# First layer's modulation vectors by unsplit float32 matmuls on column quarters, tokens loaded first

## The chip, the core and the metric

The kernel runs on one core of a Trainium2 chip. The metric is device time in microseconds, from the first to the last instruction of one launch. A core has TensorE (PE, with its weight loads listed apart as PEld), VectorE (DVE), ScalarE (ACT), GpSimd (POOL) and queues that move data from DRAM; here nearly all loads are issued by SyncE (SP).

## The reference, cut to what matters

Two transformer layers (the second of another kind than the first) are followed by two blocks with experts. Only the start of the first layer and its attention matter here. `c` and `c_ctx` are two vectors of 1024; `ada_w[i]` is 1024 x 6144. The six modulation vectors of a layer are a matrix product with only two rows:

```python
c_act = silu(c); cc_act = silu(c_ctx)
mx = split(c_act @ ada_w[i] + ada_b[i], 6)      # for the 512 tokens x
mc = split(cc_act @ ada_w[i] + ada_b[i], 6)     # for the 256 places of the context
h_x = rms_norm(x, norm1_g[i]) * (1 + mx[1]) + mx[0]
h_c = rms_norm(y_ctx, norm1_g[i]) * (1 + mc[1]) + mc[0]
out_c, out_x = windowed_gqa_sink(h_x, h_c, attn_w_qkv, ...)
x = x + mx[2] * out_x                           # mx[3], mx[4], mx[5] serve the feed-forward part
```

So nothing of the first layer's products can start before vectors 1 (scale) and 0 (shift) are there; vectors 2, 4 and 3 are needed later, in and behind the attention.

## The kernel before

All activations stand with features on the partitions: `x` is a tile of 128 x 8 x 512, `ctxT` one of 128 x 8 x 256, and tokens are worked on in groups of 256 (two of `x`, one of the context). Nearly all products are exact in float32 by splitting both operands into a high and a low float32r part (`split`: ACT makes the high part, L299, DVE the low part, L300) and adding three products of parts (L351 to L353 in `mm3`, L956 to L958 in `Attention.product`).

One `ada_w` vector (`ada_pe`, from L461) is made in two halves of 512 columns. For each half eight matmuls, one for each 128 rows of `ada_w`, take the activated vectors as the stationary operand and 128 x 512 weights as the moving one. There are two forms. With `split=True` the weights are split, the stationary operand has four columns (high and low part of both vectors, `csp`), and the matmuls are L478 and L479. With `split=False` the weights stay float32 and the stationary operand has two columns (L473). The profile shows each float32 matmul as two matmul instructions, one pass each; the program gives both forms an array shape of 128 rows by 32 columns at column 0. The result row is copied out by ACT (L482), turned by four transposes (L485), and the bias is added (L490 to L493).

At the start (from L1516) the order written is: load and compute the scale vector (chunk 1) in the split form, then issue the loads of the tokens (L1535) and the context (L1536), then the shift vector (chunk 0) in the split form with the squares and the sums of the three groups' norms between its steps (`squares` L593 and L595, `rstds` L605 to the spread at L393). When the shift vector is copied out (`take`, L1480), `Norm.gen` runs for each group and each of 8 feature tiles: a multiplication by gain and 1/rms (L623), the high part (L624), and the low part, for even tiles by L629, for odd tiles by a second pass on ACT (L626) and L627. `Attention.begin` runs beside it: it loads the first keys' and queries' weights, splits them and runs the first keys' and queries' products (`firstk`, `firstq`, `firstc`), one group after the other.

The attention then runs over 8 pairs of heads with 6 blocks each (`Attention.heads`). Between the steps of a block it takes steps of other work from a queue (`Fill.pump`), each step giving its length by `yield` (0.9 for one L473 matmul). The queue orders by rank: token values, keys, the next pair's queries, output projections (added in pairs 2, 4 and 6), and last the modulation vectors: both halves of vector 2 in pair 0, one half each of vectors 4, 4, 3, 3 in pairs 1, 3, 5, 7. The share of the queue taken in each block (`rate`) counts 7.6 for each such half. What an engine runs at which place is in the end set by a scheduler that goes by the order of writing and by when operands are ready in its own estimate.

Of the kernel before, what the change touches and what calls it, by code (L numbers as in the profile page):

```python
# [18 lines left out]
S = 512  # L19
# [75 lines left out]
def _constants():  # L95
# [22 lines left out]
    # attention rope: head_dim 64 = [r1 16 | r2 16 | c1 16 | c2 16], two heads on the partitions  # L118
# [12 lines left out]
    # window mask, keys [previous block | own | next]  # L131
# [4 lines left out]
    # retention rope: 64 row frequencies | 64 column frequencies  # L136
# [4 lines left out]
    # retention decay exponents  # L141
# [7 lines left out]
    # partial rope of the second block  # L149
# [11 lines left out]
    # pooling counts  # L161
# [6 lines left out]
    # hyena: position features, decay window, transform tables  # L168
# [15 lines left out]
    # forward [n, (cos f 0..511 | -sin f 0..511, with the Nyquist column in place of f=0)]  # L184
# [30 lines left out]
# ---------------------------------------------------------------------------  # L215
# device side
# ---------------------------------------------------------------------------
class Net:
# [22 lines left out]
    # -- small tables -------------------------------------------------------  # L241
# [14 lines left out]
    # -- weights ------------------------------------------------------------  # L256
# [27 lines left out]
    def more(self, pairs, stages=0):  # L284
        """further buffers for weights"""
# [7 lines left out]
    def split(self, v):  # L293
        """f32 [128, k, c] -> hi, lo (f32r), exactly v = hi + lo up to float32's last bit"""
# [8 lines left out]
    # -- streams beside the main one, by the time of the tensor engine -------  # L303
# [13 lines left out]
    def side(self, gen, steady=False):  # L317
        """a generator whose steps each take so long; steady: on the whole, else each of them at least"""
# [12 lines left out]
    def cpanel(self, src, k, c, some=slice(None)):  # L331
        """[128, k, c] from DRAM, as pieces of 128 columns"""
# [3 lines left out]
    def kpanel(self, src, k, c):  # L336
        """[128, k, c] from DRAM, as pieces [128, 1, c]... of at most 1024 elements, listed by k"""
# [9 lines left out]
    # -- products -----------------------------------------------------------  # L347
# [15 lines left out]
    def rsqrt(self, pool, v, n):  # L363
        """[128, n] small: 1 / sqrt(v)"""
# [4 lines left out]
        # a first guess from the exponent and three steps of Newton's  # L369
# [11 lines left out]
    def col_stats(self, ps, sq, scale, eps, pool):  # L381
        """sums of sq [128, n] over the partitions -> scale * sum + eps, tokens on the partitions [128, n / 128]"""
# [7 lines left out]
    def spread(self, ps, y, pool):  # L390
        """y [128 tokens, nb] -> the same on all partitions, tokens along the free axis, in ps [128, nb * 128]"""
# [53 lines left out]
# -- first block -------------------------------------------------------------  # L445
# [4 lines left out]
class Hidden:  # L450
    """the normalized inputs of a layer in two parts (hi, lo), features on the partitions: tokens, then context"""
# [9 lines left out]
def ada_pe(net, i, chunk, mod, stage, row, halves=(0, 1), done=None, split=True):  # L461
    """one of the six modulation vectors, for both streams, on the tensor engine, by split weights or in float32"""
    nc = net.nc
    src = net.ins["ada_w"][i].rearrange("(k p) c -> p k c", p=128)
    n = 4 if split else 2
    for j in halves:
        acc = net.ps()[:n]
        for k in range(8):
# [3 lines left out]
            if not split:  # L472
# [3 lines left out]
            if k % 2 == 0:  # L476
                h, l = net.split(w[:, k % 4:k % 4 + 2])
# [2264 lines left out]
```

## Time and profile before

| | us |
|---|---|
| median of 3 runs | 3169.13 |
| lowest and highest | 3168.89, 3169.7 |
| profiled execution, span | 3174.9 |
| first product of the attention starts (in the profiled execution) | 44.83 |
| first scores start | 91.5 |
| last pair of heads begins | 411.1 |

The profiled execution is one run of its own; its span is 5.8 us above the median. Over the whole span PE is busy 95%, DVE 64%, ACT 44%.

How to read the rows further down. A row of stretches has the stretch, its length, then for PE, PEld, DVE, ACT and POOL the busy time and the number of instructions, then the granted TensorE clock (1.00 is 2.4 GHz, 0.50 is 1.2 GHz), the DMA engines' busy share and GB/s. A row of the timeline has start, duration, engine, line, operation, output<-inputs, shapes, count (merged neighbours) and, in brackets, idle time before it and what ended it. A row of grouped instructions has line, engine, operation, names, shapes, count, then busy time, mean ns of one, and the idle time before them with its causes. Matmuls overlap in their pipeline, so their spacing is read from starts, not from durations.

### The profile page before, as it was taken

The numbers are of one execution on the slowest core, as the hardware profiler recorded it, in microseconds if no ns is written. First come the engines' busy times: TensorE is split into PE (matmuls) and PEld (weight loads), VectorE is DVE, ScalarE is ACT, GpSimd is POOL, SyncE is SP. The second block draws the span as 40 slices with busy tenths as digits, with TensorE's granted clock in tenths as the row PEclk, the third lists the DMA queues.
The fourth block names the chain that finished last, engine by engine and source line by source line (L and its number), as shares of the span: only waits on it lengthen the run. The fifth ranks groups of instructions, "written<-read, shape, count | busy, mean of one in ns | idle before, by whom it ended". The sixth has DMA issues, their size and how long they took to land. (4 is left out here: it accounts for less than half of the span.)

```text
span 3174.9 us, 45357 instructions
## 1 busy us (share of the span) xinstructions
PE 3008.7 (95%) x17640; PEld 2541.3 (80%) x17640; DVE 2021.1 (64%) x3944; ACT 1398.8 (44%) x2431; POOL 375.7 (12%) x362
## 2 busy tenths in 40 slices
PE   7999999999999999999999999989989989999996
PEld 4777779888888988888887788877878867788874
DVE  7688886445552754535465543668778666977865
ACT  6567773121212532323343322436555544645544
POOL 0011130000000200000010000211213211121211
PEclk8999999999999999999999999999999989999997
DMA  6112123334441222313133332231469943145994
GB/s 218 61 48 66 47 74 100 120 100 126 134 146 54 86 69 77 92 53 93 61 103 105 128 121 90 83 117 46 122 199 360 336 157 119 41 136 200 376 349 156
DMA packets 316336, 410.38 MB, mean 129 GB/s; under 512 B 15374, under 2 KB 263310, under 8 KB 314960
## 3 DMA queue, kind: packets, MB, share of 16 engines
q1 hardware_dynamic: 305744, 369.61, 35.5%
q0 software_dynamic: 10368, 37.75, 3.1%
q8 instruction: 144, 2.36, 0.3%
q14 instruction: 80, 0.66, 0.1%
HBM read 379.01 MB, written 28.31 MB: 128 GB/s over the span
## 5 line engine op out<-in xcount | busy, mean ns | idle before, releaser
L299 ACT ACTIVATE hi<-st 128x1024 fp32r<-128x1024 f32 (+1 forms) x436 | 449.7, 1035 | 637.6 <-PE ps L352 490.1
L300 DVE TENSOR_TENSOR lo<-st,hi 128x1024 fp32r<-128x1024 f32 (+1 forms) x436 | 531.6, 1222 | 197.7 <-ACT hi L299 191.8
L351 PE MATMUL ps<-hxh,hi 128*128 128x512 f32 (+1 forms) x1280 | 477.7, 374 | 5.0 <-DVE ctxT L756 2.1
L352 PE MATMUL ps<-hxl,hi 128*128 128x512 f32 (+1 forms) x1280 | 475.1, 371 | 0.3 <-DVE hxl L629 0.3
L353 PE MATMUL ps<-hxh,lo 128*128 128x512 f32 (+1 forms) x1280 | 474.4, 371 | 0.0
L351 PEld LDWEIGHTS ps<-hxh,hi 128*128 128x128 f32 x1280 | 241.9, 189 | 54.6 <-ACT sg L809 5.3
L353 PEld LDWEIGHTS ps<-hxh,lo 128*128 128x128 f32 x1280 | 242.1, 189 | 42.4 <-issue 1.2
L352 PEld LDWEIGHTS ps<-hxl,hi 128*128 128x128 f32 x1280 | 242.4, 189 | 40.8 <-issue 1.2
L351 PE MATMUL ps<-ah,hi 128*128 128x256 f32 (+1 forms) x592 | 200.7, 339 | 3.1 <-DVE x L756 1.9
L352 PE MATMUL ps<-al,hi 128*128 128x256 f32 (+1 forms) x592 | 198.7, 336 | 0.2 <-DVE al L361 0.2
L353 PE MATMUL ps<-ah,lo 128*128 128x256 f32 (+1 forms) x592 | 198.5, 335 | 0.0
L756 DVE SCALAR_TENSOR_TENSOR x<-ps,vecs,x 128x512 f32<-128x512 f32 (+1 forms) x136 | 84.4, 623 | 144.4 <-PE ps L353 144.0
L2517 PE MATMUL pa<-hi,xt 128*128 128x256 f32 x576 | 168.0, 292 | 0.6 <-ACT xt L360 0.5
L2519 PE MATMUL pa<-lo,xt 128*128 128x256 f32 x576 | 164.7, 286 | 0.0
L2518 PE MATMUL pa<-hi,xt 128*128 128x256 f32 x576 | 163.8, 284 | 0.0
L810 DVE TENSOR_TENSOR sg<-sg,ps 128x512 f32<-128x512 f32 (+1 forms) x70 | 40.0, 572 | 190.9 <-PE ps L353 190.6
L351 PEld LDWEIGHTS ps<-ah,hi 128*128 128x128 f32 x592 | 111.6, 189 | 19.7 <-DVE x L756 5.1
L351 PE MATMUL ps<-hi,hxh 128*128 128x256 f32 x416 | 120.9, 291 | 3.7 <-DVE hy L1953 1.1
L2543 PE MATMUL py<-st,at 128*128 128x512 f32 x272 | 122.7, 593 | 1.3 <-DVE y L2547 1.3
L352 PE MATMUL ps<-lo,hxh 128*128 128x256 f32 x416 | 119.8, 288 | 2.2 <-DVE lo L300 2.2
L352 PEld LDWEIGHTS ps<-al,hi 128*128 128x128 f32 x592 | 111.6, 189 | 12.5 <-DVE al L361 0.4
L353 PEld LDWEIGHTS ps<-ah,lo 128*128 128x128 f32 x592 | 111.5, 188 | 12.5
(651 smaller groups left out, 7755.3 us busy)
## 6 DMA issues: line engine op xcount, KB each, us to landing
st<-moe_w_dram SPq DMA_DIRECT2D x102, 1024.0 KB, 10.7
st<-ffn_w_in_dram SPq DMA_DIRECT2D x44, 1024.0 KB, 5.3
ast<-ada_w_dram SPq DMA_DIRECT2D x56, 512.0 KB, 4.6
st<-ret_w_qkvg_dram SPq DMA_DIRECT2D x24, 1024.0 KB, 5.2
st<-ffn_w_out_dram SPq DMA_DIRECT2D x24, 768.0 KB, 4.8
st<-ada_w_dram SPq DMA_DIRECT2D x12, 1024.0 KB, 5.2
st<-w_in_dram SPq DMA_DIRECT2D x12, 1024.0 KB, 7.5
ast<-ada_w_dram SPq DMA_DIRECT2D x8, 1024.0 KB, 12.6
```

The source lines that it names most:

```text
L299: self.nc.scalar.activation(h, v, AF.Copy)
L300: self.nc.vector.tensor_tensor(l, v, h.bitcast(F32), op=OP.subtract)
L351: self.nc.tensor.matmul(ps, wh, xh, start=(i == 0), stop=False)
L352: self.nc.tensor.matmul(ps, wh, xl, start=False, stop=False)
L353: self.nc.tensor.matmul(ps, wl, xh, start=False, stop=(i == n - 1))
L756: net.nc.vector.scalar_tensor_tensor(xm, p, self.gate[:, m:m + 1], xm, op0=OP.mult, op1=OP.add)
L810: nc.vector.tensor_tensor(sg, sg, pu, op=OP.mult)
L2517: nc.tensor.matmul(o, th[:, k], wh[:, kk], start=(k == 0), stop=False)
L2518: nc.tensor.matmul(o, tl[:, k], wh[:, kk], start=False, stop=False)
L2519: nc.tensor.matmul(o, th[:, k], wl[:, kk], start=False, stop=(k == 7))
L2543: nc.tensor.matmul(py[:, n * 512:n * 512 + 512], at[:, f], w2[f][:, 0, n * 512:n * 512 + 512], start=(f == 0), stop=(f == 1))
```

## The change

- `ada_pe` loses the split form. A matmul takes 32 columns as its stationary operand (`cwide[k]`: the two wanted columns and 30 that follow them in the same tile) and writes to one of four quarters of the accumulator's partitions; block k of the rows goes to quarter k mod 4, so that each quarter sums two blocks. The quarters are added, and the row turned, by four float32 matmuls with a 128 x 2 matrix of ones and zeros (`sel`) in place of the transposes. All halves of vectors 1, 0, 2, 4 and 3 are made so.
- The start issues the loads of tokens and context before any of `ada_w`. Squares and sums of the norms stand before the scale vector's steps, 1/rms within them. The multiplication by gain and 1/rms (`scaled`) stands between the scale and the shift vector. Behind the shift vector each group needs only the high and the low part (`shifted`, 8 ACT and 8 DVE instructions per group; the second ACT pass of odd tiles is gone). The first keys' and queries' weights are loaded and split behind the first group.
- In the attention a step of a modulation vector counts 0.25 for a matmul and 0.8 for the end of a half, and `rate` 2.8 for a half.

The core of the diff:

```diff
-def ada_pe(net, i, chunk, mod, stage, row, halves=(0, 1), done=None, split=True):
+def ada_pe(net, i, chunk, mod, stage, row, halves=(0, 1), done=None):
...
-            if not split:
-                nc.tensor.matmul(acc, net.cact[:, k, :], w[:, k % 4], start=(k == 0), stop=(k == 7))
-                yield 0.9
-                continue
-            if k % 2 == 0:
-                h, l = net.split(w[:, k % 4:k % 4 + 2])
-            nc.tensor.matmul(acc, net.csp[:, k, :], h[:, k % 2], start=(k == 0), stop=False)
-            nc.tensor.matmul(acc, net.csp[:, k, :], l[:, k % 2], start=False, stop=(k == 7))
-            yield 0.45
+            q = k % 4 * 32
+            nc.tensor.matmul(acc[q:q + 32], net.cwide[k], w[:, k % 4], start=(k < 4), stop=(k >= 4), tile_position=(0, q))
+            yield 0.25
...
-            nc.tensor.transpose(pt[:, m * n:m * n + n], row1[:, m * 128:(m + 1) * 128], net.ident[:n, :n])
+            nc.tensor.matmul(pt[:, m * 2:m * 2 + 2], row1[:, m * 128:(m + 1) * 128], net.sel, start=True, stop=True)
...
+    def scaled(self):
+        for k in range(8):
+            self.net.nc.vector.scalar_tensor_tensor(self.sq[:, k], self.x[:, k, self.xs], self.gain[:, k:k + 1], self.r, op0=OP.mult, op1=OP.mult)
+
+    def shifted(self):
+        nc = self.net.nc
+        for k in range(8):
+            hh, hl, s = self.hh[:, k, self.xs], self.hl[:, k, self.xs], self.shift[:, k:k + 1]
+            nc.scalar.activation(hh, self.sq[:, k], AF.Identity, bias=s)
+            nc.vector.scalar_tensor_tensor(hl, self.sq[:, k], s, hh.bitcast(F32), op0=OP.add, op1=OP.subtract)
...
-            rate = (10 * (pr < 7) + 16 * (pr in (2, 4, 6)) + 10 * (pr in (2, 7)) + 7.6 * len(beside.get(pr, ()))) / 6
+            rate = (10 * (pr < 7) + 16 * (pr in (2, 4, 6)) + 10 * (pr in (2, 7)) + 2.8 * len(beside.get(pr, ()))) / 6
...
-            ns = norms(0, 0, hid, asp, sp)
-            run(ada_pe(net, 0, 1, mod, stage, row))
-            gain(0, 0)
             for hs in HS:
                 nc.sync.dma_start(x[:, :, hs], net.ins["xT"][:, :, hs])
             nc.sync.dma_start(ctxT, net.ins["cT"])
-            shift = ada_pe(net, 0, 0, mod, stage, row)
+            ns = norms(0, 0, hid, asp, sp)
             for n in ns:
                 n.squares(asp.tile([128, 8, 256], F32, name=net.nm("xsq"), tag="xsq", bufs=3))
-                for _ in range(5 if n is ns[0] else 6):
-                    next(shift)
+            scale = ada_pe(net, 0, 1, mod, stage, row)
+            for _ in range(9):
+                next(scale)
             RmsNorm.rstds(ns, sp, asp)
-            run(shift)
+            run(scale)
+            gain(0, 0)
+            for n in ns:
+                n.scaled()
+            run(ada_pe(net, 0, 0, mod, stage, row))
             take(0, 0)
+            first = []
+            for n in ns:
+                n.shifted()
+                if n is ns[0]:
+                    first += [Attention.panel(net, c) for c in (1024, 0)]
```

## Rows read from the trace of the kernel before

**Rows 1.** Head of the page: span of the profiled execution, instructions.
```profile
span 3174.9 us, 45357 instructions
```
**Rows 2.** Stretches of the start, all engines (columns as told above).
```profile
0.00:10.00 10.00, 0.59 (x1) 0.08 (x1) 1.33 (x7) 3.32 (x4) 0.19 (x4) 1.00 0.79 256
10.00:24.00 14.00, 9.73 (x39) 3.19 (x39) 10.98 (x16) 11.13 (x17) 0.00 (x0) 0.98 1.06 377
24.00:36.00 12.00, 8.57 (x28) 4.21 (x28) 11.56 (x23) 9.25 (x12) 0.00 (x0) 0.60 1.06 374
...
44.80:65.00 20.20, 17.90 (x131) 16.09 (x131) 19.47 (x49) 17.42 (x38) 0.00 (x0) 1.00 0.28 88
...
71.00:81.50 10.50, 10.24 (x50) 10.02 (x48) 7.21 (x26) 2.06 (x3) 0.50 (x1) 0.51 0.58 200
```
**Rows 3.** Groups of instructions up to 44.8 us (columns as told above).
```profile
L300 DVE TENSOR_TENSOR lo<-ast,hi 128x1024 fp32r<-128x1024 f32 x16 | 18.9, 1221 | 6.2 <-ACT hi L299 6.2
```
**Rows 4.** Timeline of the shift vector's end, up to the first product.
```profile
42.03 0.59 ACT L482 ACTIVATE arow<-ps 4x512 f32<-4x512 f32 x1 [0.32 <-PE ps L479]
...
42.67 0.41 PE L485 MATMUL ps<-kident,arow 4*128 4x4 f32 x4 [0.46 <-ACT arow L482]
...
44.07 0.24 DVE L1480 COPY vecs<-mod 128x8 f32<-128x8 f32 x2
...
44.83 0.39 PE L956 MATMUL firstk<-hxh,hi 128*128 128x256 f32 x1 [1.75 <-ACT hxh L624]
```
**Rows 5.** Groups of instructions from 44 to 69 us: the norms' parts.
```profile
L624 ACT ACTIVATE hxh<-nt,vecs 128x256 fp32r<-128x256 f32 x16 | 7.7, 503 | 4.0 <-DVE nt L623 2.3 <-DVE vecs L1480 1.6
L623 DVE SCALAR_TENSOR_TENSOR nt<-x,gains,nps 128x256 f32<-128x256 f32 x15 | 6.9, 476 | 0.0
...
L629 DVE SCALAR_TENSOR_TENSOR hxl<-nt,vecs,hxh 128x256 fp32r<-128x256 f32 x8 | 3.9, 482 | 0.0
```
**Rows 6.** Timeline: last of the norms, last of the first products, statistics behind them.
```profile
64.45 0.43 DVE L627 TENSOR_TENSOR hcl<-nt,hch 128x256 fp32r<-128x256 f32 x1 [0.46 <-ACT nt L626]
...
67.76 0.28 PE L957 MATMUL firstc<-hcl,hi 128*128 128x256 f32 x1
67.88 0.28 PE L958 MATMUL firstc<-hch,lo 128*128 128x256 f32 x1
...
68.11 0.95 PE L972 MATMUL ps<-kblk,ol 128*128 128x2 f32 x8
```
**Rows 7.** Timeline of PE around three groups of the modulation matmuls, in the attention.
```profile
120.22 0.38 PE L1183 MATMUL po<-th,vs 128*128 128x256 f32 x1
120.53 1.02 PE L473 MATMUL ps<-st,cact 128*2 128x512 f32 x2
121.48 0.38 PE L1184 MATMUL po<-tl,vs 128*128 128x256 f32 x1
...
133.45 1.88 PE L473 MATMUL ps<-st,cact 128*2 128x512 f32 x4
```
**Rows 8.** Group of the modulation matmuls over the attention, 91.5 to 459 us.
```profile
L473 PE MATMUL ps<-st,cact 128*2 128x512 f32 x96 | 47.5, 592 | 0.0
```
**Rows 9.** Stretches: pairs of heads 1, 3, 4 and 5.
```profile
137.30:178.80 41.50, 41.42 (x228) 27.43 (x227) 31.05 (x96) 30.76 (x76) 5.14 (x7) 1.00 0.24 77
...
236.10:281.70 45.60, 45.11 (x269) 34.23 (x268) 35.92 (x102) 29.00 (x71) 5.40 (x7) 1.00 0.11 36
281.70:325.20 43.50, 41.34 (x274) 36.53 (x273) 39.06 (x109) 31.60 (x77) 5.29 (x7) 1.00 0.26 86
325.20:367.70 42.50, 41.41 (x238) 29.89 (x237) 33.57 (x96) 29.25 (x75) 5.75 (x7) 1.00 0.05 13
```
**Rows 10.** Timeline: ACT and PE beside one group of the modulation matmuls.
```profile
168.99 1.88 PE L473 MATMUL ps<-st,cact 128*2 128x512 f32 x4
...
169.09 0.58 ACT L360 ACTIVATE th<-tr 128x512 fp32r<-128x512 f32 x1
...
170.80 0.39 PE L1183 MATMUL po<-th,vs 128*128 128x256 f32 x1
```

More of the change, by code (lines that the diff above doesn't have):

```diff
@@ L611, in rstds @@
             net.spread(a.r, y[:, 2 * g:2 * g + 2], pool)
-    def gen(self):
-        if self.r is None:
-            yield 1.5
-            ps = yield from self.sums()
-            yield from self.rstd(ps, self.acc, EPS)
-            self.r = ps[:, 256:512]
+    def scaled(self):
[7 more added lines that the diff above has]
+            nc.vector.scalar_tensor_tensor(hl, self.sq[:, k], s, hh.bitcast(F32), op0=OP.add, op1=OP.subtract)
+    def gen(self):
+        yield 1.5
+        ps = yield from self.sums()
+        yield from self.rstd(ps, self.acc, EPS)
+        self.r = ps[:, 256:512]
         nc, gain, shift = self.net.nc, self.gain, self.shift
@@ L946, in t, with panel @@
         return (pool or self.ap).tile(list(shape), dt, name=self.net.nm(tag), tag=tag, bufs=bufs)
-    def panel(self, c0):
-        net = self.net
-        return net.split(net.stage(self.wq[:, :, c0:c0 + 128], 8, 128))
+    @staticmethod
+    def panel(net, c0):
+        wq = net.ins["attn_w_qkv"][0].rearrange("(k p) c -> p k c", p=128)
+        return net.split(net.stage(wq[:, :, c0:c0 + 128], 8, 128))
     def product(self, p, w, c0, n, yields=True):
@@ L1015, in keys @@
     def keys(self, j):
-        w = self.panel(1024 + j * 128)
+        w = self.panel(self.net, 1024 + j * 128)
         f, sq = self.ftiles()
@@ L1052, in queries_rest, with begin @@
         yield 0.1
-    def begin(self, before, ps_es):
+    def begin(self, first, ps_es):
         net, nc = self.net, self.net.nc
-        kw, qw = self.panel(1024), self.panel(0)
+        kw, qw = first
         wst = net.stage(self.wq[:, :, 1280:1536], 8, 256)
@@ L1061, in begin @@
         for g, (c0, n) in enumerate(GR):
-            before[g]()
             for is_k, w in ((1, kw), (0, qw)):
@@ L1466, in first_block @@
     fb = es.enter_context(net.pool("first"))
-    net.cact = fb.tile([128, 8, 2], F32, name="cact")
-    nc.scalar.activation(net.cact, net.v("c2").rearrange("p (k v) -> p k v", v=2), AF.Silu)
-    net.csp = fb.tile([128, 8, 4], F32R, name="csp")
-    nc.vector.tensor_copy(net.csp[:, :, 0:2], net.cact)
-    nc.vector.tensor_tensor(net.csp[:, :, 2:4], net.cact, net.csp[:, :, 0:2].bitcast(F32), op=OP.subtract)
+    cact = fb.tile([128, 48], F32, name="cact")
+    nc.vector.memset(cact, 0.0)
+    nc.scalar.activation(cact[:, :16], net.v("c2"), AF.Silu)
+    net.cact = cact[:, :16].rearrange("p (k v) -> p k v", v=2)
+    net.cwide = [cact[:, 2 * k:2 * k + 32] for k in range(8)]
+    net.sel = fb.tile([128, 2], F32, name="sel")
+    nc.vector.tensor_reduce(net.sel, net.ident.rearrange("p (c q) -> p q c", q=32)[:, 0:2], axis=AX.X, op=OP.add)
     mods = [fb.tile([128, 6, 8, 2], F32, name=f"mod{i}") for i in range(2)]
@@ L1536, in first_block @@
             nc.sync.dma_start(ctxT, net.ins["cT"])
[L1537 removed]
+            ns = norms(0, 0, hid, asp, sp)
             for n in ns:
                 n.squares(asp.tile([128, 8, 256], F32, name=net.nm("xsq"), tag="xsq", bufs=3))
[L1540 to L1541 removed]
+            scale = ada_pe(net, 0, 1, mod, stage, row)
+            for _ in range(9):
+                next(scale)
             RmsNorm.rstds(ns, sp, asp)
[L1543 to L1544 removed]
+            run(scale)
[3 more added lines that the diff above has]
+            run(ada_pe(net, 0, 0, mod, stage, row))
+            take(0, 0)
+            first = []
[3 more added lines that the diff above has]
+                    first += [Attention.panel(net, c) for c in (1024, 0)]
         aes = ExitStack()
         att = Attention(net, hid, x, ctxT, vecs[:, 0, 1, 0], vecs[:, 0, 1, 1], fill, aes, sp)
[L1548 to L1558 removed]
+        att.begin(first, ps_es)
         def ada(ch, j):
@@ L1562, in ada @@
             row = lambda: (late.get("pool") or att.rp).tile([128, 512], F32, name=net.nm("arow"), tag="aux")
-            return lambda: ada_pe(net, 0, ch, mod, net.stage, row, (j,), done, False)
+            return lambda: ada_pe(net, 0, ch, mod, net.stage, row, (j,), done)
         ms = ExitStack()
```

30 lines of the change are left out of this document (7 added, 23 removed).

## The prediction, made before any run of the changed kernel

> **What bounds the kernel now.** I read the page's head first [rows 1], then the stretches of the start, and asked of each what is late. Up to 36 us the load queues move 256, 377 and 374 GB/s, and the DMA engines are at or near full use [rows 2]. Both vectors (8.4 MB), the tokens and the context (3.15 MB) and the small tables (0.26 MB) are 11.8 MB, and by these rates they have passed at 10 + 14 + 10.6 = 34.6 us. So the start is bound by the load first. Then comes a tail: the shift vector's row is copied at 42.03, turned at 42.67, taken at 44.07, and the first product starts at 44.83 [rows 4]. That tail is long because the weights' split lies behind the load: 16 low parts of 1.22 us on DVE [rows 3], which also sums the squares (11.56 of 12 us busy, [rows 2]). From 44.8 to 65 us DVE is the bound, 19.47 of 20.20 us [rows 2], with the norms' instructions at 476 to 482 ns each [rows 5]. PE does its products as the tiles come, and the last of 144 starts at 67.88 and ends at 68.16 [rows 6]. From there to the first scores (91.5 us) it is a chain of the kernel's own, with a stretch at half clock (0.51 from 71 to 81.5 us, [rows 2]).
>
> In the attention PE is shown busy for nearly the whole of each pair of heads, but that is not a PE at its peak. Pair 4 has no modulation matmul and a projection, 8 x (6 x 0.24 + 6 x 0.12) = 17.3 us of matmuls at the spacing of [rows 6] (0.12 us for 256 columns, twice that for 512). Pairs 1, 3 and 5 have no projection, and 8 to 13 modulation matmuls. Pair 4 takes 43.5 us, the others 41.5, 45.6 and 42.5 [rows 9]. So the side work hardly shows in the length of a pair; it sits where PE would wait for ACT and DVE. [Rows 10] show one such place: a modulation group occupies PE from 168.99 to 170.80, and the tile that the next matmul reads is only made from 169.09 to 169.67.
>
> **The change, part by part.**
>
> (1) Loads. The same 11.8 MB pass, in another order. The first piece of `ada_w` lands behind 4.5 MB, at 10 + 1.9 MB / 377 = 15.0 us, then one piece of 1.05 MB every 2.8 us, the eighth at 34.6 us. As now, weights of keys and queries are issued beside the last pieces; I take 35.2 us, and 36 as the late bound. No queue gains a wait in front of these loads: the eighth piece needs the buffer of the first, whose matmuls are done by 18 us.
>
> (2) Splits. 16 ACT and 16 DVE instructions go, 18.9 us of DVE alone [rows 3]. They pay for the multiplications that are moved forward: 24 x 0.476 = 11.4 us of DVE [rows 5] between the scale vector (ready near 26 to 27 us) and the shift vector, done at about 38 us and so hidden; if the scale vector is 3 us later, 2 us of it show.
>
> (3) The matmuls on quarters. One float32 matmul is two passes, and two matmuls in a row take 1.88 us with a last pass of 0.59, so a pass takes 0.43 and a matmul 0.86 [rows 7]. The trace of before has no two matmuls on different quarters, so what four of them cost is bounded: 4 x 0.86 = 3.44 us if nothing overlaps, 0.86 + a little = 0.95 if all four run together, and 5 x 0.43 = 2.15 if matmuls start in order and a quarter's second pass waits for its first, so that it runs beside the next quarter's first. A joint with other matmuls costs 0.31 - 0.12 = 0.19 us before a group and 0.95 - 0.86 = 0.09 behind it [rows 7], 0.28 in all. I take 2.15, the value that follows from passes issued in order; 3.44 is the slow end, and beyond it 4 x (0.86 + 0.28) = 4.56, were each quarter a joint. The Trainium skill ("TensorE: Matmul & The Clock Gate", Part 3: Packing small matmuls) says that matmuls on different column quarters run at once, 2.38 times as fast for three of them, and that matmuls start and end strictly in order; no row here shows the first. By its factor four would take 1.4 us, an estimate, instead of my 2.15.
>
> (4) The tail behind the last piece: 2.15 + 0.17 for the end of the last pass, 0.7 for the copy (0.59 and its wait, [rows 4]), four float32 matmuls with `sel`, eight passes, as long as the eight at 0.95 us [rows 6] and 0.1, then bias, two copies and the first high part, 0.2 + 0.35 + 0.55. That is 5.2 us: first product at 40.4 instead of 44.83, 4.4 us sooner (39.2 with full overlap).
>
> (5) Norms. Behind the shift vector 24 high parts on ACT (12 us at 0.50) and 24 low parts on DVE (24 x 0.48 = 11.5), plus two splits of weights (2.1 and 2.4) and small tables (0.5): done at 39.9 + 14.4 = 54.3, against 64.88 now [rows 5, 6]. Next in line is PE: 144 x 0.12 = 16.9 us of products from 40.4, 1 us for waits on the first group, so the end is near 58.3 instead of 68.16. What follows keeps its 23.4 us. **Start: 10 us gained**, of which 4.4 is (4) and the rest (5).
>
> (6) Clock. In 24 to 36 us, with PE busy 8.57 of 12, 0.60 was granted; later 71 to 81.5 fell to 0.51 [rows 2]. That stretch, about 10 us at half clock, cost 5 us of PE time. I leave it as it is; it may go (5 us gained) or another like it may fall on the first products (5 us lost). The same page of the Trainium skill ("TensorE: Matmul & The Clock Gate", Part 1) says that the clock falls after a stretch with the engine idle; by that rule the thinner use of PE under the load speaks against the change. The 5 us either way are from the row alone.
>
> (7) Attention. 48 matmuls, 96 passes [rows 8], are 41.3 us; mostly they stand alone, so with joints up to 41.3 + 48 x 0.28 = 55. After: 48 x 0.43 = 20.6, twelve groups' joints 3.4, and the four matmuls with `sel` instead of transposes, 6 x 0.6 = 3.6. PE work falls by some 25 us (35 with full overlap, 8 with none). What comes back in time is bounded by nothing and all of it. The pairs of [rows 9] say little comes back: 17.3 against some 9 us of side work, and 43.5 us against 42.5 in pair 5, is 1 us for 8, and against pair 3 less than nothing. I take a quarter, as fewer joints also shorten the waits that ACT and DVE have for PE: **6 us**. The lower `rate` spreads queries over more blocks; that side work is cheap either way, by the same rows, and I cost it at nothing, with 4 us either way if that cover is thinner than it looks.
>
> Nothing behind the attention changes but its time. Sum: 10 + 6 = 16 us. The profiled execution would go from 3174.9 to about 3159; it lies 5.8 above the median, and I carry the difference over: 3169.1 - 16 = 3153.
>
> **Rivals.** (A) No overlap of quarters. PE needs 3.44 us for a piece that comes every 2.8, so from 15.0 us it runs 8 x 3.44 = 27.5, with some 4 us of statistics and `sel` matmuls between, to 46.5; the vector is there at 49.1 and products end at 67, 1 us sooner. The attention gains 8 us of PE work, 2 of time. Time 3166. For it: no row shows overlap. (B) The side work does cost its PE time, and it all comes back: 10 + 25 to 35, 3125 to 3134. Against it stand pair 4 and [rows 10]. (C) The gain at the start is lost before the first scores: value products and statistics that now fill PE's waits up to 68 us come behind, and a clock fall hits them; 5 at the start, 3 in the attention, 3161. (D) Slower: every quarter is a joint, 1.14 us a matmul. Then the vector waits for PE: 15.0 + 36.5 + 4 + 2.6 = 58, products end at 76, 8 late, and the attention gives nothing back: 3177. It decides from (68.2 - 15.0 - 4 - 2.6 - 17.9) / 32 = 0.90 us a matmul; alone it is 0.86. "TensorEngine Tiling (Array Packing)" in the Trainium skill (Key Properties) says that changing the tiling mode drains the engine, and changing the tile alone does not; by that D would not come.
>
> **How the numbers follow.** Forecast, overlap and a quarter back, 3144 to 3161: 0.66. A 0.14, a fifth of it beyond the bound of 0.2%, which is about what a measurement of this kernel can tell from no change (6.3 us; faster is below 3162.8). B 0.07. C 0.06. D 0.07. Faster: 0.66 + 0.07 + 0.03 of A + 0.04 of C = 0.80. Slower 0.07, same 0.13. The range goes from the forecast's low end, with the clock stretch gone and some of B, 3139, up to A, 3167.
>
> **What will show it.** The first `firstk` product near 40 us (A: 49 or later; D: 58). L624 has 24 instructions and L626 none; the last of the norms near 54; the last `firstc` near 58. Four quarter matmuls in a row start 0.43 us apart or less with overlap, 0.86 without. First scores near 81. Pairs 1, 3 and 5 shorter by 1 to 2 us each, pairs 4 and 6 not; if they lose 5 each it is B. The prediction is wrong if the start's gain is gone at the first scores, or if the pairs get longer because their blocks lack side work.

## The result, and the profile after

The change made the kernel slower: 3191.89 us (median of 4 runs, 3189.77 to 3192.66) against 3169.41 for the kernel before, measured beside it. The ratio is 1.0067, 95% interval 1.0053 to 1.0081. The prediction was 3153, range 3139 to 3167, with a chance of 0.07 for slower. It was wrong in size and in sign.

Read against the rows of before, the profiled execution of after has this course. The first scores start at 84.2 us instead of 91.5, so 7.3 us were gained at the start. The last pair's last scores end at 459.6 instead of 450.4, so 16.5 us were lost in the attention. The rest adds 6.8 us more, and the span is 3190.9 against 3174.9 [rows 1]. So the two traces show 16.0 of the 22.5 us between the medians; the traced execution of before lies above its median, and where the other 6.5 us are is not shown.

**The start.** Stretches of after (stretch, length, busy time and instructions of PE, PEld, DVE, ACT, POOL, granted clock, DMA share, GB/s), to be held against [rows 2]:

```profile
24.00:36.00 12.00, 10.49 (x71) 5.56 (x75) 4.90 (x16) 1.20 (x2) 0.00 (x0) 1.00 1.06 379
36.00:44.20 8.20, 2.58 (x17) 1.79 (x9) 6.14 (x19) 2.11 (x4) 0.00 (x0) 0.67 0.15 45
44.20:49.10 4.90, 4.43 (x19) 4.13 (x20) 4.90 (x11) 4.90 (x12) 0.00 (x0) 0.50 0.66 212
```

The clock of the first row holds from 28.6 us on only, where the trace's records of the clock begin; ahead of that PE ran at the half level, as "The start alone, repaired" shows.

The timeline of after around the shift vector's end, which answers to [rows 4]:

```profile
36.86 0.60 ACT L477 ACTIVATE arow<-ps 128x512 f32<-128x512 f32 x1 [3.09 <-PE ps L474]
...
37.91 3.22 DVE L605 SCALAR_TENSOR_TENSOR xsq<-ctxT,gains,nps 128x256 f32<-128x256 f32 x8
41.04 0.16 DVE L482 TENSOR_TENSOR mod<-ps,vec 128x8 f32<-128x8 f32 x1
...
41.35 1.84 PE L480 MATMUL ps<-sel,arow 128*128 128x2 f32 x8 [4.61 <-DVE mod L482]
...
43.42 0.24 DVE L1483 COPY vecs<-mod 128x8 f32<-128x8 f32 x2
...
44.19 0.58 PE L958 MATMUL firstk<-hxh,hi 128*128 128x256 f32 x1 [1.01 <-ACT hxh L612]
```

The load is over at 36 us as forecast, and the row is copied out at 36.86, 5.2 us sooner than before. But the `sel` matmuls that turn it wait 4.61 us, and for DVE. Not for their own operand: the two accumulators of `net.ps()` take turns, and the one that they need is read by the bias addition of the first half (L482). That one stands in DVE's queue behind all 24 multiplications (L605, 31.64 to 41.13). Meanwhile PE is idle, its clock falls (0.67 from 36 to 44.2), and the first products run at the half level (0.50 from 44.2 to 49.1).

**The attention.** One row for each kernel, from the first to the last score matmuls, before and then after:

```profile
91.50:450.40 358.90, 345.60 (x2072) 268.31 (x2072) 287.20 (x804) 247.26 (x599) 49.66 (x61) 0.99 0.18 58
```

```profile
84.20:459.60 375.40, 341.48 (x2096) 280.92 (x2095) 284.55 (x803) 245.95 (x597) 48.13 (x61) 0.95 0.17 56
```

PE's idle time grows from 358.9 - 345.6 = 13.3 us to 33.9, and the granted clock falls from 0.99 to 0.95. At 0.95 over 375 us, 0.05 x 375 = 19 us of PE time are lost to the half level, against 4 before. Groups of PE instructions in these stretches show which work went and where the idle time stands (count, busy us, mean ns, idle before them and what ended it). Before:

```profile
L1183 PE MATMUL po<-th,vs 128*128 128x256 f32 x172 | 53.2, 318 | 3.7 <-ACT th L360 2.9
L1175 PE MATMUL tr<-kident,pt 128*128 128x128 f32 x344 | 49.8, 277 | 3.3 <-ACT pt L1160 3.2
L1184 PE MATMUL po<-tl,vs 128*128 128x256 f32 x172 | 48.8, 305 | 3.3 <-DVE tl L361 3.1
...
L1133 PE MATMUL sc<-maskr,identr 128*128 128x384 f32 (+1 forms) x63 | 21.8, 346 | 0.6 <-ACT pt L1145 0.5
...
L485 PE MATMUL ps<-kident,arow 2*128 2x2 f32 x24 | 2.4, 202 | 0.1
```

After:

```profile
L1184 PE MATMUL po<-th,vs 128*128 128x256 f32 x172 | 55.0, 326 | 10.6 <-ACT th L360 8.1 <-DVE ob L1202 1.6
L1185 PE MATMUL po<-tl,vs 128*128 128x256 f32 x172 | 50.6, 313 | 6.0 <-DVE tl L361 5.7
L1176 PE MATMUL tr<-kident,pt 128*128 128x128 f32 x344 | 50.5, 280 | 7.2 <-ACT pt L1161 4.8 <-DVE tl L361 1.0 <-POOL pt L1159 1.0
...
L474 PE MATMUL ps<-st,cact 128*32 128x512 f32 x96 | 24.1, 669 | 0.2 <-DMA st<-ada_w_dram 0.2
L1134 PE MATMUL sc<-maskr,identr 128*128 128x384 f32 (+1 forms) x63 | 22.5, 357 | 3.6 <-ACT pt L1146 3.4
...
L480 PE MATMUL ps<-sel,arow 128*128 128x2 f32 x48 | 6.0, 247 | 1.6 <-ACT arow L477 1.4
```

The modulation matmuls are cheaper by 47.5 [rows 8] - 24.1 = 23.4 us, the `sel` matmuls dearer than the transposes by 3.6. That is 20 us less work, near the forecast. But the waits for the attention's own chain (`pt`, then `th` and `tl`, then `ob`, made by ACT and DVE) grew by as much: for `th` from 2.9 to 8.1, for `tl` from 3.1 to 5.7, ahead of the scores from 0.5 to 3.4.

By pairs of heads, each from its first scores to the next pair's, pairs 0 to 5 take 51.0, 51.3, 51.4, 46.0, 47.3 and 44.7 us, before 45.8, 41.5, 57.3, 45.6, 43.5 and 42.5. Pairs 0 and 1 lose 15 us, pair 2 gains 6, and pair 4, which has no modulation matmul, loses 4.

What a visit of the quarter matmuls costs is seen on PE's timeline of after, from its start to the next matmul's:

```profile
145.89 1.05 PE L474 MATMUL ps<-st,cact 128*32 128x512 f32 x2
146.87 0.38 PE L1184 MATMUL po<-th,vs 128*128 128x256 f32 x1
...
148.71 1.05 PE L474 MATMUL ps<-st,cact 128*32 128x512 f32 x4
149.69 0.39 PE L1184 MATMUL po<-th,vs 128*128 128x256 f32 x1
150.01 1.06 PE L474 MATMUL ps<-st,cact 128*32 128x512 f32 x6
151.00 0.39 PE L1185 MATMUL po<-tl,vs 128*128 128x256 f32 x1
```

One, two or three matmuls (2, 4, 6 passes) all cost 0.98 to 0.99 us at the full clock. With the visits at the half clock (1.84 to 1.85 us for one matmul) and the longer ones, there are 18, 25.0 us by their starts.

### The profile page after: what moved, and what is told of

Read it like the earlier page. It is cut to its first block, busy times and chain, and to the rows that moved or that the text cites. A ratio compares the mean times of both kernels' runs of the same rounds, so it can differ in the third digit from the quotient of the medians.

```text
span 3190.9 us, 45377 instructions
## 1 busy us (share of the span) xinstructions
PE 3006.9 (94%) x17680; PEld 2557.0 (80%) x17680; DVE 2004.1 (63%) x3924; ACT 1375.8 (43%) x2403; POOL 377.5 (12%) x362
## 5 line engine op out<-in xcount | busy, mean ns | idle before, releaser
L576 POOL TENSOR_TENSOR nacc<-nacc,nsq 128x256 f32<-128x256 f32 x56 | 50.0, 892 | 605.5 <-ACT nsq L575 597.1
```

The lines of the kernel that those rows point to most:

```text
L576: nc.gpsimd.tensor_tensor(self.acc, self.acc, sq, op=OP.add)
```

## The experiments

All results together. The ratio is to the kernel before, run beside each; attention is the stretch named above, with PE's idle time and the granted clock in it. These last four columns come from one traced execution, whose own time stands under "traced" (for before only its span is known). Those of e4 and e11 are the shortest of their kernels, 8 and 7 us below the median; that of e6 is the longest, 6 us above.

| run | median us | ratio [95%] | traced | first scores | attention | idle | clock |
|---|---|---|---|---|---|---|---|
| before | 3169 to 3172 | 1 | 3174.9 (span) | 91.5 | 358.9 | 13.3 | 0.99 |
| after | 3191.9 | 1.0067 [1.0053, 1.0081] | 3192.7 | 84.2 | 375.4 | 33.9 | 0.95 |
| e1_start_only | 3173.9 | 1.0011 [1.0001, 1.0020] | 3171.7 | 84.7 | 359.2 | 12.4 | 0.99 |
| e2_attn_only | 3192.6 | 1.0069 [1.0052, 1.0085] | 3191.7 | 92.4 | 373.5 | 33.8 | 0.95 |
| e3_one_quarter | 3192.0 | 1.0063 [1.0046, 1.0080] | 3195.2 | 85.1 | 374.2 | 19.3 | 0.98 |
| e4_pad32 | 3184.6 | 1.0044 [1.0027, 1.0060] | 3176.6 | 80.3 | 374.1 | 34.4 | 0.95 |
| e5_before_shift | 3176.6 | 1.0017 [1.0007, 1.0028] | 3179.4 | 91.3 | 357.7 | 12.0 | 0.99 |
| e6_best | 3162.5 | 0.9975 [0.9965, 0.9984] | 3168.1 | 85.7 | 359.6 | 11.5 | 0.98 |
| e7_burst | 3175.1 | 1.0014 [1.0005, 1.0024] | 3174.2 | 84.0 | 364.4 | 30.7 | 0.97 |
| e8_no_mods | 3152.1 | 0.9938 [0.9920, 0.9955] | 3152.6 | 83.7 | 347.4 | 31.8 | 0.96 |
| e9_warm | 3168.0 | 0.9991 [0.9982, 1.0000] | 3170.9 | 78.7 | 358.8 | 11.8 | 0.99 |
| e10_rate | 3176.1 | 1.0020 [1.0010, 1.0029] | 3178.7 | 83.1 | 366.3 | 28.2 | 0.95 |
| e11_burst_rate | 3175.4 | 1.0019 [1.0009, 1.0028] | 3168.4 | 82.6 | 361.3 | 29.2 | 0.96 |
| e12_warm_front | 3167.7 | 0.9985 [0.9976, 0.9994] | 3168.0 | 84.9 | 359.6 | 12.8 | 0.99 |

### Either half of the change alone

e1_start_only keeps the new start and has the old matmuls (`ada_old`) and `rate` 7.6 in the attention:

```diff
-            return lambda: ada_pe(net, 0, ch, mod, net.stage, row, (j,), done)
+            return lambda: ada_old(net, 0, ch, mod, net.stage, row, (j,), done)
```

> The changed kernel's start (tokens first, quarters, first norm during the load), but the five modulation vectors of the attention are made as in the kernel before: one unsplit float32 matmul after the other on two rows, with the old rate of side work (7.6 a vector). Theory T1 (the loss sits in the attention, where the cheaper quarter matmuls leave TensorE idle and its granted clock falls): the start keeps its gain of 7 us at the first scores (84 against 91.5 us), the pairs last what they lasted before (45.8, 41.5, 57.3, 45.6, 43.5, 42.5 us), half-clock time from 92 to 490 us goes back from 44 us to 14 to 20 us, and the time is 3160 to 3166 us, faster than the kernel before by 3 to 9 us. Rival R1 (the pairs drift because everything behind the start is ordered or timed otherwise, whatever the modulation's matmuls are): pairs of 46 to 51 us, as in the changed kernel, and 3180 us or more. Rival R2 (the late part, behind 490 us, loses 7 us on its own by the shifted addresses or the clock): 3165 to 3173 us.

e2_attn_only is the kernel before with only the attention's part of the change (`ada_quarters`: quarters, `sel`, steps and `rate`):

```diff
-            return lambda: ada_pe(net, 0, ch, mod, net.stage, row, (j,), done, False)
+            return lambda: ada_quarters(net, 0, ch, mod, net.stage, row, (j,), done)
```

> The mirror image: the start of the kernel before (split weights, tokens later), and in the attention the quarter matmuls with the rate 2.8 of the changed kernel. T1: first scores at 91 to 92 us as before, pairs of 46 to 51 us, some 30 us more at half clock between 92 and 490 us than before, drift of +16 us at the attention's end, and 3180 to 3200 us. R1: pairs as before and 3165 to 3173 us. If quarters and start only lose together, both this run and the one with the start alone are near 3169 us.

e1's attention lasts 359.2 us, its six first pairs 45.8, 41.5, 55.5, 45.6, 45.9, 42.2. e2's lasts 373.5, and e2 alone has the whole slowdown (1.0069). So the loss is in the attention, and it comes with the attention's part of the change (form, steps and `rate` together), not with the start (R1 falls). But e1 is 8 to 14 us later than T1 said: the 7 us of its start are not in its time. That is nearest to R2 (3165 to 3173 us), and the next two runs took it up.

### A tile of 32 bytes

The change dropped a tile of 32 bytes per partition (`as4`) among the constants. By it the residual, the hidden pair and the weights' ring moved from addresses 32 above a multiple of 64 to multiples of 64. e4 puts a dummy of that size into after, e5 into before, where it does the reverse:

```diff
     nc.vector.memset(net.one, 1.0)
+    net.pad = cp.tile([128, 8], F32, name="pad")
+    nc.vector.memset(net.pad, 0.0)
```

> The changed kernel with a dummy tile of 32 bytes per partition among the constants, which puts the large buffers behind it back on the addresses they had in the kernel before (the change removed a tile of that size). Nothing else differs but one small memset at the start. Rival R2 (addresses): the drift of +7 us between 490 and 2050 us goes, and the time is 3183 to 3187 us. If addresses do nothing: 3189 to 3194 us, and the drift there stays, a matter of the clock that was granted.

> The kernel before with one dummy tile of 32 bytes per partition added among the constants: the same instructions but for one small memset, with the residual, the hidden pair and the weight ring at addresses that are a multiple of 64 bytes, as in the changed kernel, and no longer 32 above one. Rival R2 (the addresses are a second cost of the change, beside the attention): the first 490 us as before, then a slow drift of +7 to +10 us between 550 and 2650 us, and 3175 to 3180 us. If the addresses are nothing: 3166 to 3172 us and no drift.

Two marks on DVE's timeline, in the second layer's vectors and at the end of the retention part, bound a stretch in which all kernels run the same instructions. Before:

```profile
543.96 0.17 DVE L521 TENSOR_TENSOR mod<-ps,vec 128x8 f32<-128x8 f32 x1 [0.41 <-PE ps L519]
...
1557.34 1.28 DVE L1408 SCALAR_TENSOR_TENSOR of<-mu,of 128x512 f32<-128x512 f32 x2
```

e5_before_shift:

```profile
543.03 0.17 DVE L523 TENSOR_TENSOR mod<-ps,vec 128x8 f32<-128x8 f32 x1 [0.41 <-PE ps L521]
...
1559.77 1.28 DVE L1410 SCALAR_TENSOR_TENSOR of<-mu,of 128x512 f32<-128x512 f32 x2
```

After:

```profile
553.00 0.17 DVE L510 TENSOR_TENSOR mod<-ps,vec 128x8 f32<-128x8 f32 x1 [0.41 <-PE ps L508]
...
1569.68 1.28 DVE L1409 SCALAR_TENSOR_TENSOR of<-mu,of 128x512 f32<-128x512 f32 x2
```

The stretch lasts 1013.4 us in before, 1016.7 in e5 and 1016.7 in after. From the first mark to the last squares of that part, 1.4 us later, it is 1017.9 to 1018.1 in the four kernels with the moved addresses (after, e1, e3, e5) and 1012.8 to 1016.1 in the ten with the old ones. So the addresses do cost time, though less than the 7 to 10 us expected: 2 to 5 us in this stretch, with the granted clock at 1.00 in all fourteen, and 5.4 us (2.2 to 8.9) for e5 as timed. e4's ratio is 0.0023, or 7 us, below after's, and its 3184.6 us lie where the address rival put them. Its trace does not show where these 7 us are, for it is that of a shorter execution, whose clock was up sooner. Which of the moved buffers does it was not tried.

### The attention: clock, dose, visits, or work

e3_one_quarter lets all eight matmuls of a half sum on one quarter, so that none overlap; steps and `rate` are after's.

```diff
-            nc.tensor.matmul(acc[q:q + 32], net.cwide[k], w[:, k % 4], start=(k < 4), stop=(k >= 4), tile_position=(0, q))
+            nc.tensor.matmul(acc[:32], net.cwide[k], w[:, k % 4], start=(k == 0), stop=(k == 7))
```

> The changed kernel, but in the attention all eight matmuls of a half accumulate on one quarter of the columns, so that no two run at once: the same operands, steps and rate (2.8) as the changed kernel, only more time on TensorE (eight times 0.86 us or more instead of 1.9 us for a half, some 50 us more over five vectors). T1 (clock): the extra work fills idle stretches and holds the clock up, so at least half of the 50 us is paid for and the time is no later than the changed kernel's 3192 us, 3175 to 3190 us, with half-clock time from 92 to 490 us of 14 to 25 us. Rival R3 (the smaller rate alone spreads the other side work otherwise, and costs the 16 us): pairs of 46 to 51 us plus the added work, 3195 to 3240 us.

e10_rate takes the other side of it: quarters as they are, and the larger dose of side work for each block.

```diff
-... + 2.8 * len(beside.get(pr, ()))) / 6
+... + 7.6 * len(beside.get(pr, ()))) / 6
```

> The changed kernel with the 32-byte dummy tile, and the rate of side work for a modulation half put back from 2.8 to the 7.6 of the kernel before: the quarter matmuls and everything else as they are, only that each block of a pair with a modulation half is given more side work, so that the early blocks of the pair get theirs sooner and the late ones are left with none. R3 (the smaller dose for each block leaves the softmax's chain over ScalarE and VectorE uncovered): idle of the attention falls from 34 us by 8 us or more, attention of 360 to 367 us against 374, and 3171 to 3178 us against 3184.6 for the changed kernel with the dummy tile. T1 in its plain form (less work, so more idle and a lower clock, wherever it is put): 371 to 377 us and 3181 to 3188 us.

e7_burst yields once for eight quarter matmuls, e11 does both:

```diff
-            yield 0.25
+        yield 2.0
```

> The changed kernel with the 32-byte dummy tile, and in the attention all eight quarter matmuls of a half issued in one step (1.92 us), where the changed kernel breaks them into 17 visits of 1 to 2.7 us, 25.0 us in all for six halves; that is 12 to 13 us less work on TensorE over the attention. T1 (the attention cannot use the TensorE time that is set free: it comes back as waiting for ScalarE and VectorE, and as time at half clock): attention of 365 us or more (with the changed kernel 375, before 359) and 3178 to 3190 us, idle time up. Rival D (TensorE is the bound, and the visits are what the attention lost): attention of 360 to 363 us and 3170 to 3173 us.

> Both at once: eight quarter matmuls in one step and the rate 7.6. The single steps' gains add up if they are different costs (visits on TensorE, 13 us of work; the dose of side work): attention of 350 to 358 us, 3163 to 3170 us. If the attention keeps what it has lost whatever the dose: 362 us or more, as with the bursts alone (364 us), and 3173 to 3178 us.

e8_no_mods leaves the attention's modulation products out, and counts 0.1 for each half in `rate`:

```diff
-            return lambda: ada_pe(net, 0, ch, mod, net.stage, row, (j,), done)
+            def none():
+                nc.vector.tensor_copy(mod[:, ch, 4 * j:4 * j + 4], net.v("ab0", ...)...)
+                yield 0.1
+            return none
...
-... + 2.8 * len(beside.get(pr, ()))) / 6
+... + 0.1 * len(beside.get(pr, ()))) / 6
```

> The changed kernel with the 32-byte dummy tile, and without the modulation matmuls in the attention: the three vectors made there (their loads, products and transposes) are left out and the bias alone stands for them, so all of that work, 45 us on TensorE in the kernel before, is gone. If TensorE's work bounds the attention: it lasts 359 - 45 - 5 = 310 to 315 us and the kernel 3120 to 3125 us. T1 (much of that work ran in time that the softmax's chain over ScalarE and VectorE left open, and held the clock): attention of 335 us or more, with over 40 us of idle and more half-clock time than the 6.8 us of before, and 3145 us or more.

The attention's rows of e3, e7, e8, e10 and e11, in this order:

```profile
85.10:459.30 374.20, 354.95 (x2096) 279.07 (x2095) 287.33 (x803) 247.86 (x597) 48.87 (x61) 0.98 0.17 56
```

```profile
84.00:448.40 364.40, 333.72 (x2096) 275.94 (x2094) 287.49 (x803) 245.52 (x597) 49.07 (x61) 0.97 0.17 57
```

```profile
83.70:431.10 347.40, 315.57 (x1953) 269.43 (x1952) 285.68 (x791) 242.91 (x592) 50.70 (x61) 0.96 0.08 27
```

```profile
83.10:449.40 366.30, 338.08 (x2096) 278.23 (x2095) 286.44 (x803) 246.15 (x597) 48.17 (x61) 0.95 0.18 57
```

```profile
82.60:443.90 361.30, 332.11 (x2096) 276.71 (x2094) 286.40 (x803) 246.37 (x597) 48.41 (x61) 0.96 0.18 58
```

**Work is not the bound.** e8 leaves out all of the attention's modulation work, 50 us of PE in before (47.5 and 2.4). Its attention is 11.5 us shorter, not 50: idle time is 31.8 us (I had put it over 40) and the clock 0.96. So 38 of the 50 us did not come back: 18.5 of them turned into idle time, and some 10 into PE time lost to the half clock. But e8 has less of the dose too, the share of other side work that each block is given (`rate` 0.1 for a half, 7.6 in before), and the next runs show that the dose costs time by itself. So 11.5 us is what leaving the work out gained at that dose; what it would gain at the larger one no run shows. (e8's median also has the start's gain in it.)

**The dose costs, and so does the order of the visits.** Against e4 (374.1) the larger dose gives 7.8 us back in the traces, the burst 9.7, both 12.8. As timed, by the ratios, they give 7.6, 9.5 and 7.9 us: both together are worth no more than either alone, and e11's 361.3 are those of its shortest execution. So e11 came out as I had put it for an attention that keeps what it lost (3173 to 3178 us), not for gains that add up. e10 is in R3's ranges for time and attention, though idle time fell by 6.2 us and not by 8. e7's 3175.1 us lie between T1 and D. With the larger dose the attention is still 7.4 us longer than in before: the dose is about half of e4's 15.2. The burst's cause is not the one that I put down: the scheduler broke the bursts up again (15 visits, 19.1 us by their starts, where 11.5 were expected), so part of its gain must come from other places in the order, which I did not separate.

**The clock alone does not decide.** T1 was that the falling clock takes the gain back. e10 has the same 0.95 as e4 and is 7.8 us shorter. e3 has the clock up (0.98) and the same 374 us, but its modulation matmuls are back at 48.4 us of PE. It does this old amount of work under the new dose and steps, and is 15.0 us longer than e1, with old work, old dose, old steps and old transposes (some 4 us less than `sel`), at 0.98 against 0.99. So the falling clock goes with the idle time, and costs PE time, but the attention comes out slow with it and nearly without it. My forecast for e3 missed on both sides: 3192 us is above T1's bound and below R3's. How much of the 16 us is the clock's own stays open, for no run here holds the clock and leaves the order alone.

### The start alone, repaired

e6_best is e1 with the old addresses, and with the multiplications written behind the shift vector:

```diff
-            for n in ns:
-                n.scaled()
             run(ada_pe(net, 0, 0, mod, stage, row))
             take(0, 0)
+            for n in ns:
+                n.scaled()
```

> The part of the change that was seen to gain, alone: its start (tokens first, quarters, norm during the load), the old one-after-the-other modulation matmuls with rate 7.6 in the attention, the 32-byte dummy tile that keeps the old addresses, and the 24 multiplications of the norm put on VectorE's queue behind the shift vector's bias additions and no longer ahead of them. Theory T4 (those multiplications held up the shift vector): the first product of the attention near 40 us and no longer at 44.2, first scores at 76 to 80 us (before: 91.5), attention 359 us as before, no drift behind it, 3153 to 3160 us. If the bias additions were not what the shift vector waited for: first scores at 80 to 84 us and 3160 to 3164 us. If addresses do nothing, 3165 us or more.

It is the fastest complete kernel of the study: ratio 0.9975. But the first scores are at 85.7, not 76 to 80. Timeline of e6_best, PE and DVE:

```profile
33.92 5.57 DVE L631 SCALAR_TENSOR_TENSOR xsq<-x,gains,nps 128x256 f32<-128x256 f32 x14
39.74 0.17 DVE L484 TENSOR_TENSOR mod<-ps,vec 128x8 f32<-128x8 f32 x1 [0.25 <-PE ps L482]
...
39.63 3.64 PE L476 MATMUL ps<-ast,cact 128*32 128x512 f32 x16
44.05 1.87 PE L482 MATMUL ps<-sel,arow 128*128 128x2 f32 x8 [0.78 <-ACT arow L479]
```

The wait for DVE is gone (0.78 for the row's copy instead of 4.61 for the bias), but no trace shows that the repair did this. The scheduler still put 14 multiplications ahead of the first bias addition and the other 10 ahead of the second. And e3, whose start is after's, unrepaired, waits as little (e1 as well, 0.79), and has its first product sooner, at 46.17 (46.93 in e6):

```profile
43.30 1.87 PE L480 MATMUL ps<-sel,arow 128*128 128x2 f32 x8 [0.77 <-ACT arow L477]
```

What bounds the start in these executions is the clock: sixteen passes take 3.64 us here, 1.92 at the full level, and they take 3.64 up to the last half. The stretches' clock column says 1.00 there, but only because the clock's records begin at its first rise (52.3 us here, 28.6 in after, 23.1 in e4, 13.1 in before); the durations tell the level. Among the kernels with after's start the first product comes at 41.42 where the clock rose first (23.1, e4) and at 46.17 where it rose last (51.4, e3). The repair's own gain stays open: e6 is timed 11 us below e1, and the addresses are 2 to 9 us of that. e9_warm adds matmuls of no use in PE's waits, e12_warm_front keeps only those ahead of the first load:

```diff
+            def warm(n):
+                for _ in range(n):
+                    nc.tensor.matmul(wp[:, :128], net.ones, net.ones, start=True, stop=True)
+            warm(28)
```

> The kernel of the run before that was faster than both (start of the change, old modulation matmuls in the attention, old addresses, multiplications behind the bias additions), with small matmuls of no use (float32, 128x128, 0.26 us each at full clock, written to a bank that nothing reads) on TensorE where it waits in the start: 28 of them ahead of the first modulation matmul, two ahead of each sum's transposing matmuls, two behind these, six behind the last. Theory T5 (what the start lost is the clock: by the durations of its matmuls, x16 in 3.64 us, TensorE ran at the half level until 52.3 us in the run without them, and until 23 to 51 us in the other runs of the changed start, against 13 to 15 us with the start of the kernel before): the sixteen passes of a half take 1.92 us from the first one on, the shift vector is there at 38 to 39.5 us, first product at 39 to 41, first scores at 75 to 79 us, and 3152 to 3157 us. Rival (the start is bound by its loads, and the clock costs nothing there): first scores at 83 to 86 us, 3160 to 3164 us.

> The run before but one kept the 28 matmuls of no use ahead of the first modulation matmul, and two to eight more around each half; there the first scores came 7 us earlier (78.7 us, 85.7 without any), yet the whole was no faster (3168 against 3162 us): by its trace it gave back 10 us between 1550 and 2050 us, where it had more time at half clock. Here only the 28 ahead of the first modulation matmul are left. T5 (the clock's first rise is what counts): first rise of the clock before 10 us, first scores at 77 to 81 us. For the whole: if the start's 7 us arrive at the end unless a particular run of clock falls takes them, 3154 to 3159 us; if an earlier start is given back behind 1550 us here too, 3162 to 3169 us, with drift of +8 us or more between 1550 and 2050 us.

e9_warm, PE and DVE:

```profile
34.20 2.17 PE L476 MATMUL ps<-ast,cact 128*32 128x512 f32 x16
...
37.15 1.05 PE L483 MATMUL ps<-sel,arow 128*128 128x2 f32 x8 [0.78 <-ACT arow L480]
...
40.51 0.16 DVE L486 TENSOR_TENSOR mod<-ps,vec 128x8 f32<-128x8 f32 x1
```

e12_warm_front, stretches:

```profile
14.00:51.40 37.40, 31.48 (x137) 18.28 (x138) 22.27 (x61) 11.16 (x23) 0.00 (x0) 0.50 0.73 265
51.40:84.90 33.50, 32.93 (x262) 32.35 (x262) 24.69 (x65) 17.23 (x32) 3.60 (x2) 0.95 0.32 101
```

With the waits filled, the halves take 1.93 to 3.08 us and the first scores come at 78.7, 7 us sooner than in e6: the half clock did hold up the start. In e12 the clock rose at 7.1 us, fell at 13.9 when the useless matmuls had ended and PE waited for the tokens' squares, and came back at 51.4; first scores at 84.9. So what counts is that the clock stays up, not that it rose once; my expectation for e12 was wrong. In e9, with the clock up, DVE's queue holds the last bias addition behind the multiplications, from 38.2 (`sel` done) to 40.51; there it is DVE again that comes last.

The 7 us of e9 are not in its time, 3168.0 us where 3152 to 3157 were expected: 0.9991 against 0.9975 for e6, whose intervals just touch. In its trace it gives back 10 us between 1550 and 2050 us against the trace of before, e6 and e12 some 6. By the starts of the same PE instructions, e6 and e12 have that back at 2860 us (9.0 and 9.6 us ahead of before, 8.1 and 8.9 at 545 us), and e9 has not (5.5 ahead, 15.3 at 545). Stretches at half clock fall there in other places from kernel to kernel. Why an earlier start fares worse there is open, and so is the order of e6, e9 and e12 among themselves.

## Why the prediction was wrong, step by step

- **(1) Loads:** right. The last quarter matmuls end at 36.73, with the last piece taken at 35.2 in the forecast; in e4, where PE came sooner, it waited for that piece until 33.73 (second line under (3)).
- **(2) Multiplications hidden on DVE:** wrong, in two ways. The scale vector was ready at 31.5, not at 26 to 27, since PE at the half clock did the norm's sums and spreads ahead of its second half (28.8 in e4, with the clock up at 23.1). And I named no wait behind them: the bias additions queue behind the 24, and the second half's accumulator waits for the first half's bias. I had 2 us of cost for "3 us later"; it was 4.6 us of PE's waiting in after's trace, and 0.8 in e1 and e3, where the half clock made PE later than DVE.
- **(3) Quarters:** overlap is full. Four matmuls take 1.07 us alone (first line below, from e4), eight 1.92, against 0.86 for one; I took 2.15 for four, and my fast end, 0.95, was nearer. The Trainium skill ("TensorE: Matmul & The Clock Gate", Part 3: Packing small matmuls) gives 2.38 times for three column tiles; here it is 4 x 0.86 / 0.96 = 3.6 times for four, so its sign was right and the 1.4 us estimated from it still too long. In the attention the price is by visit, not by matmul: 0.98 us for one to three matmuls at the full clock.

```profile
32.04 1.07 PE L476 MATMUL ps<-ast,cact 128*32 128x512 f32 x8
33.73 1.94 PE L476 MATMUL ps<-ast,cact 128*32 128x512 f32 x8 [0.63 <-DMA ast<-ada_w_dram]
```

- **(4) and (5) Tail and norms:** the first product came at 44.19, not 40.4 (the wait of step 2), the norms ended at 55.5, not 54.3, and the last `firstc` near 64, not 58.3. Of the 5.7 us there, 3.8 are the later first product; the first 4.9 us of products ran at half clock (0.50), 2.5 us. (144 x 0.12 is also 17.3, not the 16.9 of the sum.) The start gained 7.3 us instead of 10, and only 3.9 of them by the path that I forecast: the products end at 64.27 instead of 68.16. The other 3.4 were luck, for what follows took 19.9 us and not the 23.4 that I kept, at a clock of 0.83 instead of 0.78:

```profile
68.16:91.50 23.34, 19.75 (x124) 19.05 (x124) 14.77 (x42) 8.02 (x14) 2.16 (x1) 0.78 0.27 91
```

```profile
64.27:84.20 19.93, 19.41 (x136) 19.02 (x136) 11.32 (x37) 7.92 (x14) 0.00 (x0) 0.83 0.32 106
```

- **(6) Clock:** I left it as it is, with 5 us either way, for the start alone. In the attention it went from 0.99 to 0.95, and in the start the traces of other kernels with the same instructions had it up at 23 us (e4) or only at 51 (e3). The Trainium skill (the same page, Part 1) says that the clock falls after the engine has idled; after's rows agree (PE idle from 36.7 to 41.35, 0.67 from 36 to 44.2, then 0.50), and I had quoted it as speaking against the change, but gave it no price in the attention.
- **(7) Attention:** this step failed. The work that went was sized well (25 us forecast, 20 measured). What came back was "bounded by nothing and all of it" and taken as a quarter, 6 us, so that no loss stood in the sum; it was minus 16.5 us. From [rows 9] I read that side work hardly shows in a pair's length, which agrees with e8 (11.5 of 50 us, at its smaller dose). The conclusion to draw was that taking it away hardly gains, and that its other uses (covering the waits in [rows 10], keeping PE busy) are lost: the 20 us less of work are met by 20.6 us more of idle time, and the clock falls. Of the smaller `rate` I said "I cost it at nothing, with 4 us either way"; alone it is 7.8 us (e10 against e4), half of the loss. The other half was not taken apart.
- **Not in the prediction at all:** the 32-byte tile, 2 to 9 us.

In ratios the parts sum up within their intervals: attention alone +0.0069 (e2), the start alone with the moved addresses +0.0011 (e1), together +0.0080 against +0.0067 measured. Of the rivals none came; D, the slow one, had each quarter a joint in the start, where quarters overlapped fully. The last line of "What will show it" (pairs longer because their blocks lack side work) is what e10 shows for half of the loss, and it had no chance of its own.

## What to carry to other kernels

Side work that runs in another chain's waits is largely paid for already: before making it cheaper, take it out in a trial and see what that gains (here 11.5 us of 50). Hold the dose by which the schedule hands out the other work while you do so: it changed here with the size of the work, and alone cost 7.8 us. Where an engine works off its queue in order, as DVE did here (the bias addition at 41.04 behind 24 multiplications), ask for each moved block of instructions which small ones now stand behind it, and which buffer those hold.

## What the runs showed of the hardware that I had not expected

- A visit of float32 matmuls of 512 columns on column quarters costs 0.98 to 1.00 us from its start to the next matmul's, for one to four of them at full clock.
- The clock can stay at the half level through a stretch where PE is shown busy 31.48 of 37.40 us (e12, 14.0 to 51.4), and the first rise came anywhere from 23 us (e4) to 51 (e3) in kernels whose start has the same instructions, but for one small memset (one trace of each).
- Moving large buffers by 32 bytes, from 32 above a multiple of 64 bytes to a multiple of 64, costs about 2 to 5 us in 1014: all four kernels with the moved addresses took 1017.9 to 1018.1 us, all ten others 1012.8 to 1016.1, at a granted clock of 1.00 in each.
